# A hybrid decoder layer in float32 on one core: where the weight sums of the up projection are made, and the hand-over to the down projection

## The chip, the cores and the metric

The kernel runs on one core of a Trainium2 chip. A core has five engines that run side by side and meet only through semaphores: TensorE (PE in the profile, its weight loads PEld), VectorE (DVE), ScalarE (ACT), GpSimd (POOL) and SyncE (SP). Sixteen DMA engines move data between the chip's memory and the core's on-chip memory. Each engine takes its instructions in the order of its own queue.

The metric is the device time of one execution in microseconds (us). The profile is of one execution; its span runs from the first to the last instruction.

## The reference

One layer of a decoder on a residual stream of 1024 tokens by 1024 channels, all in float32: a norm and an input projection, a pooling mixer and a recurrent head group side by side, an output projection, a squared-ReLU MLP of width 4096, a gated embedding and a final norm.

```python
z = rms_norm(h, norm_mix_g[l])
proj = z @ w_in[l]
...
h = h + jnp.concatenate([y_pool, y_lru], axis=-1) @ w_out[l]
z = rms_norm(h, norm_mlp_g[l])
h = h + jnp.square(jax.nn.relu(z @ w_up[l])) @ w_down[l]
z = rms_norm(h, norm_ple_g[l])
gate = jax.nn.sigmoid(z @ w_ple_gate[l] + b_ple_gate[l])
h = h + gate * (p[l] @ w_ple_proj[l])
...
return rms_norm(h, norm_final_g)
```

The change lies in the MLP, the line with `w_up` and `w_down`.

## The kernel before, in words

**Arithmetic.** A float32 product is made from three passes of TensorE. Each operand is split into a high and a low part (`split`, lines 185 and 186: ScalarE copies the high part into the type that TensorE reads fast, VectorE subtracts it and leaves the low part), and TensorE adds high x high, high x low and low x high (`mm`, line 358).

**The up projection** works on 16 pairs of output tiles (`NPAIR`). For each pair the 2 x 2 block product of activations and weights is made with seven products instead of eight (the Strassen-Winograd scheme), called P1 to P7. Each product is four blocks of the contraction by three passes, 12 matmuls of 128x128 by 128x512. The scheme needs sums of the weight blocks A11, A12, A21 and A22 of each pair:

- P1 takes A11 and P2 takes A12 as they are, from the tile `a`; P4 takes A22 as it is, from a half of `T[5]`.
- P5 takes the running sum `chain` (the first half of the tile `c`), which starts as A21 + A22. Then A11 is added to it for P6, and then A12 for P3.
- P7 takes A21 + A11, the second half of `c`.

(The signs of the scheme are in the order of the blocks and in the sums of the activations.) In the kernel before, all four sums are made by DMAs that add what they read to what is already in the on-chip tile (`grow`, line 227). Such DMAs are issued by GpSimd (the queue POOLq), plain loads by SyncE (SPq).

**Loading.** `load_up(m)` issues, for pair m, the load of A21 into both halves of `c` (line 243), the accumulation of A22 and A11 onto them (512 KB), the load of A11 and A12 into `a` (line 248) and of A22 into `T[5]` (line 249). There are two sets of tiles `a` and `c`; for even pairs they come from a rotating pool (`wu_raw` in the profile), for odd pairs they are two fixed tiles (`wu`). In the kernel before, `load_up(m + 2)` is asked for at the split of P4 of pair m. For the last pair the weight of P3 has a tile of its own, `T[4]`, filled by one load and three accumulating DMAs (line 251 and `grow`).

**Order.** `UP` lists the products. From pair 2 on a pair runs P1, P5, P4 of the pair before (written P4' here), P6, P2, P3, P7. `weights()` hands out a split weight and asks for one further on in the list, so splits are made ahead of their products. The split weights take four slots in rotation (`up_place` and the two buffers of `wp`). The splits keep their order among themselves; the other instructions are placed by a scheduler, which also may put a DMA earlier than the source does.

**Within a pair** (`up_open`, `up_fourth`, `up_pair`): P1 goes to the bank `ps_a_u`, and a ScalarE copy (line 911) starts the bank `ps_b_u` with its negative, on which P6, P7 and later P4 are added. ScalarE copies of finished banks are at line 852, VectorE's subtractions at line 874. When P4 of a pair is done, `finish_up` applies ReLU, the norm's factor and the square (lines 833 and 835), makes the sums that the down projection's scheme needs (line 218) and stores everything to memory in four DMAs (lines 846 and 847).

**Last pair and the down projection.** `up_last` runs the last pair. On the way `preload_down` and `open_down` load the first weights (line 293) and the first operands `X` of the down projection (line 299, `wd<-act`). `open_down` gives up the space `y`, in which the operands of P1, P2 and P3 lie, and opens the space `wd` at its place; `X` are its first four tiles. A space opened like this waits for all readers of what lay there before. The down projection then runs 2 chunks of seven products by four parts, all of `ps_P_d`.

Of the kernel before, what the change touches and what calls it, by code (L numbers as in the profile page):

```python
# [8 lines left out]
F32 = mybir.dt.float32  # L9
# [3 lines left out]
ALU = mybir.AluOpType  # L13
# [35 lines left out]
NPAIR = DFF // P // 2  # L49
# [14 lines left out]
def block_kernel(  # L64
# [17 lines left out]
    nc = tc.nc  # L82
    pool = ctx.enter_context(tc.tile_pool(name="pool", bufs=1))
# [13 lines left out]
    A = [a_pair(i) for i in range(NT)]  # L97
    spaces = {}

    def space(name, n, dt, side="left"):  # L100

        spaces[name] = ExitStack()
        sb = spaces[name].enter_context(tc.tile_pool(name=name, bufs=1, side=side))
        return [sb.tile([P, S], dt, name=f"{name}{i}") for i in range(n)]

    def leave(name):
# [8 lines left out]
    T = [t_all[:, i] for i in range(6)]  # L115
# [16 lines left out]
    def bank(name):  # L132
        return pd.tile([P, HALF], F32, tag="pd", name=name)
# [4 lines left out]
    HALVES = FIRST, SECOND = slice(0, HALF), slice(HALF, S)  # L138
# [43 lines left out]
    def split(src, hi, lo, g=None, eng=None):  # L182

        if g is None:
            first = pin(nc.scalar.activation(hi, src, AF.Copy))  # L185
            lowest[:] = [pin((eng or nc.vector).tensor_tensor(lo, src, f32(hi), ALU.subtract)).ins]  # L186
        else:
            first = pin(nc.scalar.activation(hi, src, AF.Identity, scale=g))
            lowest[:] = [pin(nc.vector.scalar_tensor_tensor(lo, src, g, f32(hi), ALU.mult, ALU.subtract)).ins]
        upper[:] = [first.ins]  # L190
        return first.ins

    def raw_tile(name):
        return wp.tile([P, S], F32, tag="raw", name=f"{name}_raw")
# [22 lines left out]
    def dv(op, to, x, y):  # L217
        return nc.vector.tensor_tensor(to, x, y, op).ins

    up_raw, up_lower, up_spare, up_place = {}, {}, [], itertools.cycle(("whi", "wlo"))  # L220
    A22, A11, A12, A21 = (slice(n * HALF, (n + 1) * HALF) for n in range(4))

    def twice(x):
        return x.unsqueeze(1).broadcast_to([P, 2, x.shape[-1]])

    def grow(to, src):
        nc.gpsimd.dma_start(to, src, accum_op=ALU.add)
# [9 lines left out]
    def load_up(m):  # L237

        a, c = [raw_tile(f"wu{m}_{i}") for i in range(2)] if m % 2 == 0 else up_spare
        up_raw[m] = a, c, T[5][:, HALVES[m % 2]], c[:, FIRST] if m else R[:, SECOND]  # L240
        w = w_up[m]
        if m:
            nc.sync.dma_start(c.rearrange("p (y s) -> p y s", y=2), twice(w[:, A21]))
            grow(c, w[:, : 2 * HALF])
        else:
            nc.sync.dma_start(c[:, SECOND], w[:, A21])
            grow(c[:, SECOND], w[:, A11])
        nc.sync.dma_start(a, w[:, A11.start : A12.stop])
        nc.sync.dma_start(up_raw[m][2], w[:, A22])
        if m == NPAIR - 1:  # L250
            nc.sync.dma_start(T[4][:, FIRST], w[:, A21])
            for x in (A22, A11, A12):
                grow(T[4][:, FIRST], w[:, x])

    FIRST_UP = "P6", "P7", "P4", "P5", "P1", "P2", "P3"
    UP = [(0, kind) for kind in FIRST_UP]
    for m in range(1, NPAIR - 1):
        UP += [(m, "P1"), (m, "P5")] + [(m - 1, "P4")] * (m > 1) + [(m, kind) for kind in ("P6", "P2", "P3", "P7")]
    m = NPAIR - 1
    UP += [(m, "P1"), (m, "P5"), (m, "P2"), (m, "P3"), (m - 1, "P4"), (m, "P4"), (m, "P6"), (m, "P7")]  # L260

    def up_weight(m, kind):
        first, last = m == 0, m == NPAIR - 1
        if first and kind == "P6":
            load_up(0)
        a, c, a22, chain = up_raw[m]
        src = {
            "P1": a[:, FIRST], "P2": a[:, SECOND], "P4": a22, "P5": R[:, FIRST] if first else chain,
            "P6": chain, "P7": c[:, SECOND], "P3": T[4][:, FIRST] if last else chain,
        }[kind]  # L270
        w = wp.tile([P, S], F32R, tag=next(up_place), name=f"wu{m}_{kind}")
        hi, lo = (w[:, hs] for hs in HALVES)
        split(src, hi, lo)
        up_lower[m, kind] = lowest[0]
        if kind == "P5" and not first:
            grow(chain, w_up[m][:, A11])
        elif kind == "P6" and not last:
            grow(chain, w_up[m][:, A12])
        elif kind == ("P4", "P3")[first] and m < NPAIR - 2:
            load_up(m + 2)  # L280
        elif first and kind == "P7":
            load_up(1)
        return hi, lo

# [59 lines left out]
    def weights():  # L344
        ask()
        return asked.pop(0)
# [169 lines left out]
    for k in range(NT):  # L516
# [3 lines left out]
        for hs in halves:  # L520
            if k == hs.start == 0:
                whi, wlo = (t[:, :HALF] for t in weight_tiles("wl0"))
                g = col("g_mix", 0)
                x, zhi, zlo = (t[:, hs] for t in (H[0], *A[0]))
# [9 lines left out]
            x, zhi, zlo = (t[:, hs] for t in (H[k], *A[k]))  # L534
# [18 lines left out]
        if k < 2:  # L553

            zhi, zlo = A[k]
            for hs in HALVES:
# [4 lines left out]
                for n, o in kinds:  # L561
                    w, z = ((whi, zhi), (whi, zlo), (wlo, zhi))[n]
# [57 lines left out]
    def lru_gates(o):  # L620


        hi, lo = hl(0), hl(2)
        ct, rt, _ = LSETS[o % 2]
        zhi, zlo = B[4 + o]
        ps = [psum(f"ps_g{h}{o}") for h in range(2)]
        halves = [
            [(hs.start + n, x[:, n : n + HALF]) for hs, x in parts for n in range(0, hs.stop - hs.start, HALF)]
            for parts in ps
        ]  # L630
        for n, (w, z) in enumerate(((hi, zhi), (hi, zlo), (lo, zhi))):
            for (at, x0), (_, x1) in zip(*halves):
                for r, x in zip(HEADS, (x0, x1)):
                    nc.tensor.matmul(
                        x, w[r, o * P : (o + 1) * P], turns(z[r, at : at + HALF]), start=n == 0, stop=n == 2
                    )

        with tc.issue_after(newest[0]):
            for dst, b, rows in ((rt, "ga_b", HEADS), (ct, "gx_b", HEADS[::-1])):
                for h, r in enumerate(rows):  # L640
                    for hs, part in ps[h]:
                        last = nc.scalar.activation(
                            by(dst[HEADS[h], hs], part), got(part[r]), AF.Sigmoid, bias=col(b, o)[r]
                        )
        nc.vector.tensor_tensor(H[o], H[o], ct, ALU.mult)
        return last.ins
# [76 lines left out]
    last = lru_gates(1)  # L723
# [10 lines left out]
    last = lru_gates(3)  # L734
# [3 lines left out]
    last = lru_scan(1, last)  # L738
# [130 lines left out]
    def up_product(m, kind, ps, ts=range(4), w=None, more=False):  # L869
        product(ps, w or weights(), lambda t: up_operand(kind, t), ts, more=more)  # L870
# [33 lines left out]
    def up_open(m):  # L904

        cc, c11, c12, c21, c22 = up_sums(m)
        a, d = bank(f"ps_a_u{m}"), bank(f"ps_d_u{m}")
        up_product(m, "P1", a)
        if m < NPAIR - 1:
            chains[m] = banks(f"ps_b_u{m}")[:, :HALF]  # L910
            nc.scalar.activation(chains[m], a, AF.Copy, scale=-1.0)  # L911
        else:
            copy(c12, a)
        up_product(m, "P5", d)
        copy(c22, d)
        return a, d

    def up_fourth(m):
        cc, c11, c12, c21, c22 = up_sums(m)
        ps = chains.pop(m)  # L920
        up_product(m, "P4", ps, more=True)
        copy(c21, ps)
        return finish_up(m, cc)
# [21 lines left out]
    def up_last():  # L945
        m = NPAIR - 1
        cc, c11, c12, c21, c22 = up_sums(m)
        preload_down()
        a, d = up_open(m)
        up_product(m, "P2", a, more=True)  # L950
        copy(c11, a)
        up_product(m, "P3", d, more=True)
        first = open_down()
        store_up = up_fourth(m - 1)
        with tc.issue_after(first):
            store_up()
        ps = bank(f"ps_P4_u{m}")
        up_product(m, "P4", ps)
        load_w(0, 0, 3)
        copy(c21, ps)  # L960
        ps = bank(f"ps_P6_u{m}")
        up_product(m, "P6", ps)
        prepare(0, 0)
        take(c12, ps, c12)
        dv(ALU.subtract, c22, c12, c22)
        add(c21, c12)
        take(c12, d, c12)
        ps = banks(f"ps_P7_u{m}")[:, :HALF]
        up_product(m, "P7", ps)
        for tp in range(1, NQ):  # L970
            prepare(0, tp)
        add_both(cc[:, 1].rearrange("p (y s) -> p y s", y=2), ps)
# [8 lines left out]

    def open_down():
        leave("y")
        tiles = space("wd", 8, F32)
        late = space("wd1", 4, F32, "right")
        early.append(space("w0", 2, F32R))
        X[:] = tiles[:NQ]
        for q in range(NQ):
            W[1, q], W[3, q] = late[q], tiles[NQ + q]
        for tp in range(NQ):  # L990
            last = load_x(0, tp)
        load_w(0, 0, 2)
        for q in range(2):
            load_w(0, 1, q)
        return last.ins
# [330 lines left out]
    for g, hs in enumerate(GROUPS):  # L1326
# [3 lines left out]
        for n, o in enumerate(ORDER[g]):  # L1330
# [14 lines left out]
            if g == 0 and 1 <= n < 5:  # L1345
                raw = wp.tile([P, S], F32, tag="raw", name=f"wg0_{n + 3}_raw")
                nc.sync.dma_start(raw, w_gate[n + 3])
                x = slice((n - 1) * P, n * P)
# [142 lines left out]
```

## Time and profile before

| what | us |
|---|---|
| three runs: lowest, median, highest | 1016.5, 1017.62, 1021.67 |
| the profiled execution, its own time | 1016.62 |
| its span, first to last instruction | 1014.9 |
| mean TensorE clock granted | 0.972 of full |

How to read the profile: PE is TensorE's matmuls, PEld its weight loads, which lie beside them. L358 is line 358 of the kernel. `out<-in` names the tiles, with their numbers left out, so `ps_b_u` stands for the bank of every pair. An arrow with an engine and a line after an idle time names what ended that idle time. The number after the time in a group is the mean length of one instruction in ns.

The page also gives the span in 40 slices of 25.4 us, each digit the busy share of an engine in tenths (9 is 90% or more), PEclk the granted clock:

```profile
PE   9999999999797878787879799999999999999996
PEld 7888888888676757575667587888888888888885
DVE  7998885486544434343434369889987668888865
ACT  7469954374333423333333255443434344656322
POOL 4300001001111111101010100000000000000001
PEclk9999999999898989898989899999999999999999
```

The up projection lies in slices 9 to 24, the down projection in slices 25 to 36.

### The profile page before, as it was taken

The page shows a single profiled execution, that of the slowest core. Times are in us where ns is not written, and L with a number is a line of the kernel's source. Part 1 is how long each engine was busy: PE and PEld are TensorE (multiplying, and loading weights), DVE is VectorE, ACT ScalarE, POOL GpSimd, SP SyncE. Part 2 cuts the span into 40 slices and gives each one's busy share as a digit, 9 for nine tenths or more (in the row PEclk, how much of TensorE's full clock was granted, in tenths as well). Part 3 has the DMA queues.
Part 4 walks back from the last instruction along what each step waited for, and adds up shares of the span by engine and source line. Part 5 has one row for each costly group of instructions (what it writes and reads, how often), then busy time and mean ns, then how long its engine had stood idle before and what let it go on. Part 6 is the DMA issues. An engine that isn't in the chain of part 4 may idle for free.

```text
span 1014.9 us, 11314 instructions
## 1 busy us (share of the span) xinstructions
PE 939.7 (93%) x4227; PEld 802.5 (79%) x4227; DVE 681.8 (67%) x819; ACT 464.8 (46%) x606; POOL 68.8 (7%) x87
## 2 busy tenths in 40 slices
PE   9999999999797878787879799999999999999996
PEld 7888888888676757575667587888888888888885
DVE  7998885486544434343434369889987668888865
ACT  7469954374333423333333255443434344656322
POOL 4300001001111111101010100000000000000001
PEclk9999999999898989898989899999999999999999
DMA  7210263146665566566665679946653234013263
GB/s 255 84 52 32 83 200 96 46 100 153 163 187 166 167 165 166 166 166 165 166 166 166 165 238 335 341 146 187 217 193 125 83 125 146 21 64 103 54 192 117
DMA packets 61766, 151.38 MB, mean 149 GB/s; under 512 B 5520, under 2 KB 10512, under 8 KB 61712
## 3 DMA queue, kind: packets, MB, share of 16 engines
q1 hardware_dynamic: 54224, 133.10, 39.4%
q0 software_dynamic: 7488, 17.57, 10.6%
q8 instruction: 33, 0.54, 0.2%
q14 instruction: 21, 0.17, 0.1%
HBM read 114.99 MB, written 35.65 MB: 148 GB/s over the span
## 4 chain that ended last, share of the span: by engine, by line
PE 63%; DMA 21%; DVE 7%; issue 5%; ACT 3%; POOL 1%; SPq 0%; DVEq 0%; POOLq 0%; ACTq 0%
PE ps_P_d L358 28%; DMA wu<-in_w_up 10%; DMA wu_raw<-in_w_up 9%; PE ps_i L358 8%; PE ps_o L358 8%; PE ps_e L358 7%; DVE t_h L833 3%; PE ps_l L358 3%; DVE wu_P L186 2%; ACT wu_P L185 1%; PE ps_b_u L358 1%; ACT t_h L835 1%; PE ps_a_u L358 1%; PE ps_P_u L358 1%; PE ps_l L565 1%
## 5 line engine op out<-in xcount | busy, mean ns | idle before, releaser
L358 PE MATMUL ps_P_d<-a,wd_P_hi 128*128 128x512 f32 x880 | 261.7, 379 | 0.0
L358 PE MATMUL ps_b_u<-a,wu_P 128*128 128x512 f32 x504 | 135.7, 424 | 54.4 <-ACT ps_b_u L911 54.4
L358 PEld LDWEIGHTS ps_P_d<-a,wd_P_hi 128*128 128x128 f32 x880 | 166.3, 189 | 23.6
L358 PEld LDWEIGHTS ps_b_u<-a,wu_P 128*128 128x128 f32 x504 | 105.1, 213 | 79.2 <-ACT ps_b_u L911 59.7
L358 PE MATMUL ps_P_d<-a,wd_P_lo 128*128 128x512 f32 x440 | 166.8, 379 | 0.0
L186 DVE TENSOR_TENSOR wu_P<-wu_raw,wu_P 128x512 fp32r<-128x512 f32 x45 | 30.9, 688 | 103.3 <-ACT wu_P L185 103.3
L358 PEld LDWEIGHTS ps_P_d<-a,wd_P_lo 128*128 128x128 f32 x440 | 83.2, 189 | 11.8
L186 DVE TENSOR_TENSOR wu_P<-wu,wu_P 128x512 fp32r<-128x512 f32 x47 | 32.3, 687 | 80.2 <-ACT wu_P L185 80.2
L358 PE MATMUL ps_a_u<-y,wu_P 128*128 128x512 f32 x360 | 84.8, 384 | 0.0
L185 ACT ACTIVATE wu_P<-wu_raw 128x512 fp32r<-128x512 f32 x45 | 27.9, 621 | 116.6 <-DMA wu_raw<-in_w_up 116.3
L358 PEld LDWEIGHTS ps_a_u<-y,wu_P 128*128 128x128 f32 x360 | 68.3, 192 | 12.4 <-DVE wu_P L186 2.5
L185 ACT ACTIVATE wu_P<-wu 128x512 fp32r<-128x512 f32 x47 | 29.0, 621 | 93.5 <-DMA wu<-in_w_up 88.2
L186 DVE TENSOR_TENSOR a<-wd,a 128x1024 fp32r<-128x1024 f32 x56 | 67.2, 1219 | 1.8 <-ACT a L185 1.5
L358 PE MATMUL ps_i<-a,wi_hi 128*128 128x512 f32 x256 | 66.1, 381 | 0.0
L358 PE MATMUL ps_o<-y,wo_hi 128*128 128x512 f32 x256 | 65.7, 379 | 0.0
L815 DVE TENSOR_TENSOR t_h<-t_h,ps_P_d 128x512 f32<-128x512 f32 (+1 forms) x56 | 42.5, 759 | 34.0 <-PE ps_P_d L358 34.0
L185 ACT ACTIVATE a<-wd 128x1024 fp32r<-128x1024 f32 x56 | 58.1, 1049 | 13.1 <-PE ps_P_d L358 7.0
L358 PEld LDWEIGHTS ps_i<-a,wi_hi 128*128 128x128 f32 x256 | 48.1, 189 | 8.0 <-issue 0.7
L358 PEld LDWEIGHTS ps_o<-y,wo_hi 128*128 128x128 f32 x256 | 48.4, 189 | 6.9
L358 PE MATMUL ps_d_u<-y,wu_P 128*128 128x512 f32 x180 | 45.2, 397 | 9.2 <-ACT wu_P L185 6.3
L185 ACT ACTIVATE wd_P_hi<-wd 128x1024 fp32r<-128x1024 f32 x24 | 25.3, 1054 | 52.6 <-PE ps_P_d L358 52.5
L358 PEld LDWEIGHTS ps_d_u<-y,wu_P 128*128 128x128 f32 x180 | 34.1, 195 | 18.9 <-ACT wu_P L185 8.3
(263 smaller groups left out, 1572.4 us busy)
## 6 DMA issues: line engine op xcount, KB each, us to landing
wd<-act SPq DMA_DIRECT2D x56, 512.0 KB, 5.5
act<-t_h SPq DMA_DIRECT2D x32, 512.0 KB, 5.9
wu<-in_w_up SPq DMA_DIRECT2D x16, 512.0 KB, 5.0
act<-wu SPq DMA_DIRECT2D x16, 512.0 KB, 6.2
wd<-in_w_down SPq DMA_DIRECT2D x16, 512.0 KB, 5.8
wu_raw<-in_w_up SPq DMA_DIRECT2D x15, 512.0 KB, 5.4
t_h<-in_xT SPq DMA_DIRECT2D x14, 512.0 KB, 4.6
wg_raw<-in_w_gate SPq DMA_DIRECT2D x10, 512.0 KB, 3.3
```

What stands on the lines that cost most here:

```text
L185: first = pin(nc.scalar.activation(hi, src, AF.Copy))
L186: lowest[:] = [pin((eng or nc.vector).tensor_tensor(lo, src, f32(hi), ALU.subtract)).ins]
L358: ins = nc.tensor.matmul(ps, w, turns(z[:, hs]), start=first and z is zhi and w is whi, stop=last and w is wlo, skip_group_check=more,)
L565: nc.tensor.matmul(ps, kblk(w, o), turns(z[:, hs]), start=k == n == 0, stop=False)
L815: (eng or nc.vector).tensor_tensor(to, to if y is None else y, x, ALU.add)
L833: nc.vector.scalar_tensor_tensor(cc, cc, 0.0, twice(R), ALU.max, ALU.mult)
L835: nc.scalar.activation(x, x, AF.Square)
```

## The change

It touches the loading of the up projection's weights, the order of the last pair and the opening of the space `wd`.

- `load_up` no longer loads A22 except for the first two pairs; a new function `load_a22` does. `load_up(m + 2)` is asked for at the split of P7 of pair m (at P3 for the first pair), `load_a22(m + 2)` at the split of P4, as before.
- After the split of P5, VectorE adds A11 to `chain` from the tile `a`; after the split of P6 it adds A12. The two accumulating DMAs that did this are gone. The other two sums (A21 + A22 and A21 + A11) stay accumulating DMAs in `load_up`.
- For the last pair VectorE makes `T[4]` from `chain` and A12; its four DMAs are gone.
- In the last pair P4 of the pair before comes ahead of P2 and P3, and with it that pair's finish; the stores of that finish are still issued behind the loads of `X`.
- The space `wd` is opened with waits by tile instead of by pool: each of its tiles waits for the readers of what lay at its own place.

```diff
-    def space(name, n, dt, side="left"):
+    def space(name, n, dt, side="left", waits="pool"):
 
         spaces[name] = ExitStack()
-        sb = spaces[name].enter_context(tc.tile_pool(name=name, bufs=1, side=side))
+        sb = spaces[name].enter_context(tc.tile_pool(name=name, bufs=1, side=side, reuse_waits=waits))
         return [sb.tile([P, S], dt, name=f"{name}{i}") for i in range(n)]
...
         nc.sync.dma_start(a, w[:, A11.start : A12.stop])
-        nc.sync.dma_start(up_raw[m][2], w[:, A22])
-        if m == NPAIR - 1:
-            nc.sync.dma_start(T[4][:, FIRST], w[:, A21])
-            for x in (A22, A11, A12):
-                grow(T[4][:, FIRST], w[:, x])
+        if m < 2:
+            load_a22(m)
+
+    def load_a22(m):
+        nc.sync.dma_start(T[5][:, HALVES[m % 2]], w_up[m][:, A22])
...
-    UP += [(m, "P1"), (m, "P5"), (m, "P2"), (m, "P3"), (m - 1, "P4"), (m, "P4"), (m, "P6"), (m, "P7")]
+    UP += [(m, "P1"), (m, "P5"), (m - 1, "P4"), (m, "P2"), (m, "P3"), (m, "P4"), (m, "P6"), (m, "P7")]
...
         if kind == "P5" and not first:
-            grow(chain, w_up[m][:, A11])
+            dv(ALU.add, chain, chain, a[:, FIRST])
+            if last:
+                dv(ALU.add, T[4][:, FIRST], chain, a[:, SECOND])
         elif kind == "P6" and not last:
-            grow(chain, w_up[m][:, A12])
-        elif kind == ("P4", "P3")[first] and m < NPAIR - 2:
-            load_up(m + 2)
-        elif first and kind == "P7":
+            dv(ALU.add, chain, chain, a[:, SECOND])
+        if m < NPAIR - 2:
+            if kind == ("P7", "P3")[first]:
+                load_up(m + 2)
+            if kind == ("P4", "P3")[first]:
+                load_a22(m + 2)
+        if first and kind == "P7":
             load_up(1)
...
         a, d = up_open(m)
+        store_up = up_fourth(m - 1)
         up_product(m, "P2", a, more=True)
         copy(c11, a)
         up_product(m, "P3", d, more=True)
         first = open_down()
-        store_up = up_fourth(m - 1)
         with tc.issue_after(first):
             store_up()
...
         leave("y")
-        tiles = space("wd", 8, F32)
+        tiles = space("wd", 8, F32, waits="tile")
         late = space("wd1", 4, F32, "right")
```

## The prediction

> **What bounds the kernel now.** I began with the page's busy times: PE has 93% of the span, so only the places where it stands can give anything. Next came the windows of the stages: busy time of PE, its weight loads, VectorE, ScalarE and GpSimd in a stretch, then TensorE's clock, the DMA engines' share and GB/s.
>
> ```profile
> PE 939.7 (93%) x4227; PEld 802.5 (79%) x4227; DVE 681.8 (67%) x819; ACT 464.8 (46%) x606; POOL 68.8 (7%) x87
> ...
> core 0: us, PE busy (x) PEld busy (x) DVE busy (x) ACT busy (x) POOL busy (x), PEclk, DMA share, GB/s
> 224.60:608.36 383.76, 320.09 (x1350) 265.01 (x1349) 175.79 (x224) 140.53 (x231) 40.07 (x46) 0.93 0.64 171
> 448.98:498.10 49.12, 37.47 (x157) 30.63 (x155) 19.64 (x25) 15.54 (x27) 4.38 (x5) 0.93 0.65 171
> 585.00:600.00 15.00, 15.00 (x69) 12.67 (x69) 8.93 (x14) 9.02 (x15) 0.86 (x1) 1.00 0.68 213
> 600.50:615.00 14.50, 12.26 (x58) 10.41 (x57) 12.61 (x15) 8.88 (x10) 0.00 (x0) 1.00 0.91 324
> 614.20:901.00 286.80, 286.79 (x1329) 251.07 (x1330) 236.61 (x237) 130.63 (x141) 0.00 (x0) 1.00 0.50 164
> ```
>
> The down stage (the last row) is dense: 286.80 / 1329 = 0.2158 us a matmul. The up stage (from 224.60) is not. Its 16 pairs hold 16 x 7 products x 12 matmuls = 1344, and with 4 matmuls of the norm 1348 x 0.2158 = 290.9 us. It takes 383.76, so 92.9 us are lost there. The row from 448.98 is two pairs, 24.56 us each, where 84 x 0.2158 = 18.1 would do. A dense product is 12 x 0.2158 = 2.59.
>
> Who makes PE wait is in the groups by line and form of TensorE (busy, mean ns, idle before, releaser) and in the waits:
>
> ```profile
> L358 PE MATMUL ps_b_u<-a,wu_P 128*128 128x512 f32 x504 | 135.7, 424 | 54.4 <-ACT ps_b_u L911 54.4
> L358 PE MATMUL ps_d_u<-y,wu_P 128*128 128x512 f32 x180 | 45.2, 397 | 9.2 <-ACT wu_P L185 6.3 <-ACT t_h L852 2.8
> ACT wu_P L185 <- DMA wu_raw<-in_w_up: 116.3, 14, 13.2
> ACT wu_P L185 <- DMA wu<-in_w_up: 88.2, 13, 9.5
> ```
>
> PE names a ScalarE copy (L911), but that copy reads a product long finished. One pair in the timeline shows why it is late (start, duration, in brackets the idle time before):
>
> ```profile
> 406.61 0.38 SPq L243 DMA_DIRECT2D wu<-in_w_up  x1
> 407.10 1.99 SPq L846 DMA_DIRECT2D act<-t_h  x2
> 411.71 0.32 SPq L846 DMA_DIRECT2D act<-wu  x1
> 412.13 0.88 POOL L227 DMA_DIRECT2D wu<-in_w_up  x1 [14.19 <-DVE wu L218]
> 412.69 1.23 POOL L227 DMA_DIRECT2D wu_raw<-in_w_up  x1
> 414.25 2.75 PE L358 MATMUL ps_b_u<-a,wu_P 128*128 128x512 f32 x12
> 422.67 0.63 ACT L185 ACTIVATE wu_P<-wu_raw 128x512 fp32r<-128x512 f32 x1 [12.61 <-DMA wu_raw<-in_w_up]
> 423.20 0.58 ACT L911 ACTIVATE ps_b_u<-ps_a_u 128x512 f32<-128x512 f32 x1
> 423.83 4.91 PE L358 MATMUL ps_b_u<-a,wu_P 128*128 128x512 f32 x12 [6.83 <-ACT ps_b_u L911]
> 446.29 2.86 PE L358 MATMUL ps_b_u<-a,wu_P 128*128 128x512 f32 x12 [2.00 <-ACT ps_b_u L911]
> ```
>
> The sum for P6 (chain + A11) is an accumulating DMA on GpSimd's queue. At 412.13 that queue serves the 512 KB sum of a later pair, and this pair's sum comes behind it at 412.69. ScalarE sits on the P6 split until 422.67, with L911 behind it in its queue, and PE with both. So **the up stage is bound by the landing of accumulating DMAs inside the pair**.
>
> The loss has two halves. Idle before matmuls is 54.4 + 9.2 = 63.6 us; the other 29.3 are slow matmuls after a stall. After 6.83 us idle, twelve take 4.91; after 2.00 they take 2.86, near the dense 2.75. Here the Trainium skill bears ("TensorE: Matmul & The Clock Gate", section "What's actually happening"): about 3.4 us idle halves the clock until PE has been busy as long, and the trace agrees with its 4.91 and 2.86.
>
> **The change, part by part.**
>
> *Two sums on VectorE.* Both in-pair accumulating DMAs go (two in each of pairs 1 to 14, one in the last: 29). In their place stand 30 VectorE additions of 128x512 from tiles already in SBUF. Their nearest row is the same shape on the same engine:
>
> ```profile
> L218 DVE TENSOR_TENSOR wu<-t_h 128x512 f32<-128x512 f32 x16 | 11.0, 685 | 0.0
> ```
>
> So 2 x 0.69 = 1.4 us a pair. VectorE does 19.64 us in two pairs; with the additions 22.4 of 36.3, or 62%. They are covered by VectorE's idle time if they run early. They can: four weight slots rotate, so a split may start once the product four places before it has ended. At a dense PE, P5's split may start 5.2 us before its pair, the first addition follows at once, and P6's split may start at 0, when P6 itself is due at 7.8. P3's split may start at 5.2 and P3 is due at 12.9. Without that cover, the chain split, subtract, add (0.63 + 0.69 + 0.69 = 2.0 us) twice would be bare: 4.0 us a pair.
>
> *The load a pair ahead.* The DMAs for pair m+2 (the first half's twofold load, its 512 KB accumulation on GpSimd, and the A11/A12 tile) are now asked for at P7 of pair m instead of P4 of m in the next pair. A22 alone stays with P4. Prices, from the DMA issues (count, KB, us to landing), from the view of these tiles, and VectorE's longest instruction from the timeline:
>
> ```profile
> wu<-in_w_up SPq DMA_DIRECT2D x16, 512.0 KB, 5.0
> wu<-in_w_up POOLq DMA_DIRECT2D x8, 512.0 KB, 8.5
> DMA to landing us min/median/max: 3.2/5.9/10.4
> ...
> 403.69 2.29 DVE L833 SCALAR_TENSOR_TENSOR t_h<-t_h,rstd 128x2048 f32<-128x2048 f32 x1
> ```
>
> With t = 0 at the pair's P1, P7's split starts at 7.8 (P4' has ended) and, behind a 2.29 us VectorE instruction, ends by about 12. The load lands at 12.4 + 5.0 = 17.4, the accumulation at 17.4 + 0.9 + 8.5 = 26.8. P5 of m+2 must begin to split at 36.3 + 2.6 - 1.3 = 37.6. That is **10.8 us of slack**; with both landings at the longest seen, 10.4, still 3.9. So DMA latency leaves the path. On SP the loads pass the four stores of a pair's finish. At 406.61 SP already issues the load ahead of those stores, so I cost the move at 0; at worst SP holds them from 407.10 to 411.71, 4.6 us, which the slack covers. On GpSimd's queue only one accumulation a pair is left, so none stands behind another.
>
> *Bytes.* Two pairs moved 49.12 us x 171 GB/s = 8.40 MB; four 256 KB sums fewer make 7.35 MB, in 36.3 us 203 GB/s. The row 585 to 600 shows 213 GB/s at a clock of 1.00 and a share of 0.68. No bound.
>
> *The last pair's sum, T[4].* Four DMAs become one VectorE addition. Before, the scheduler put them early, in the way of pair 1:
>
> ```profile
> 248.33 0.86 POOL L227 DMA_DIRECT2D t_h<-in_w_up  x1 [4.28 <-DMA t_h<-in_w_up]
> 248.89 1.20 POOL L227 DMA_DIRECT2D wu<-in_w_up  x1
> 256.87 4.54 PE L358 MATMUL ps_d_u<-y,wu_P 128*128 128x512 f32 x12 [2.76 <-ACT t_h L852]
> ```
>
> Pair 1's second sum stood behind one of them, and P3 of pair 1 started late by 2.76. This is inside the 92.9.
>
> *Last pair reordered, space handed over tile by tile.* P4' moves ahead of P2 and P3. The first down operands (X) overlay the tiles that P1 and P2 read.
>
> ```profile
> 595.41 2.75 PE L358 MATMUL ps_d_u<-y,wu_P 128*128 128x512 f32 x12
> 598.00 2.75 PE L358 MATMUL ps_b_u<-a,wu_P 128*128 128x512 f32 x12
> 598.19 1.90 SPq L299 DMA_DIRECT2D wd<-act  x3
> 608.36 2.97 PE L358 MATMUL ps_P_d<-a,w 128*128 128x512 f32 x13
> 611.20 1.22 DVE L218 TENSOR_TENSOR wu<-t_h,wu 128x1024 f32<-128x1024 f32 x1
> 614.21 1.56 PE L358 MATMUL ps_P_d<-a,w 128*128 128x512 f32 x6 [2.24 <-DVE a L186]
> ```
>
> Before, the X loads waited for the end of P3 (598.0), with four products, 10.4 us, to the down stage. After, they can go during P2, with P3, P4, P6, P7 and part of P2 to come: 10.4 to 12 us. Without the tile-wise wait the reorder would leave three products, 7.8. The stores and sums of pair 14 (the 611.20 row) also come two products earlier, out of the way of the X splits. What they delayed is the stop after 16 matmuls: 608.36 + 16 x 0.2158 = 611.8 to 614.21, 2.4 us. If the X loads do not move, in the busiest stretch of the DMAs (share 0.91), these 2.4 stay.
>
> **The sum.** 92.9 + 2.4 = 95.3 us can go. I leave 1.0 at the start of down and 2.3 in the stage for waits that a dense stage still has; the weight loads' short waits for VectorE's half of a split bound these:
>
> ```profile
> PEld ps_b_u L358 <- DVE wu_P L186: 2.7, 8, 0.3
> PEld ps_d_u L358 <- DVE wu_P L186: 2.6, 6, 0.4
> PEld ps_a_u L358 <- DVE wu_P L186: 2.5, 8, 0.3
> ```
>
> They are 7.8 together, 0 at the other end, and I take the part nearer to 0, since splits would run three products ahead. That saves 92.0. The profiled execution took 1016.62 (span 1014.9 and 1.7 around it), 1.0 under the median of the three runs. Forecast: 1016.6 - 92.0 = **924.6 us**.
>
> **The rivals.**
>
> *The stall shrinks but stays (0.24).* Something in the in-order queues still comes late each pair: ScalarE, whose splits, copies and squares share one queue, or the X-to-VectorE-to-ScalarE chain of the sums. For it: the bare chain is 4.0 us, and L911 has only the 5.2 us of P5 and P4' as cover. Against it: ScalarE does 15.54 us in two pairs, under half of 36.3, and its long waits were all for DMAs. With 2.0 us a pair over 14 pairs, 28: 953. With 4.0, 56, and the clock falls too: at 4.91 against 2.75 that is 2.2 a pair more, 87 together, 1012. By the rule of the Trainium skill named above, only gaps over its window pay this second part.
>
> *The stall only changes its place (0.04).* If P5 waits for its load as long as P6 did for its sum, the time stays within 0.5%, 1012 to 1022. Against it: the slack of 10.8 us.
>
> *Slower: the load falls behind the stores of the wrong pair (0.06).* SP serves in order, and the order is the scheduler's. If the load for m+2 stands behind the four stores of pair m itself, which can't be ready until P4' in pair m+1, each pair becomes a loop: P4' ends, 8.0 us of finish (403.69 to the last store at 411.71), 14.4 of load and accumulation, 1.3 of split, P5 and P4', 5.2. That is 28.9 us a pair against 24.56: 14 x 4.3 = 61 us slower, some 1078, with slow matmuls more. It decides once SP issues the load over 24.56 - 14.4 - 1.3 - 5.2 = 3.7 us after P4' has ended. Against it: at 406.61 SP issued the load before the stores although the source asked for it later than now.
>
> *The handover does nothing:* 2.4 of the sum stay; within the forecast's own range.
>
> **How the numbers follow.** Forecast 0.66 (range of its own 917 to 936: all 95.3 gone is 921.3, and runs of this kernel spread by some us; above, the 7.8 and the 2.4 stay). The range must take most of the first rival too, to about 958 (just over 2 us a pair); that leaves out the upper part of it, 0.08, and the last two, 0.10: 917 to 958. Half a per cent, 5 us, is about what a measurement of this kernel tells from no change. Faster by more: 0.66 + 0.24 = 0.90; within: 0.04; slower: 0.06.
>
> **What the profile will show.** If right: the up stage takes about 293 us, its clock reads 1.00, the wait of PE for L911 is under 5 us, ScalarE's waits for weights from w_up are nearly gone, VectorE's group of additions has 30 more, GpSimd one accumulation a pair, and the first down product starts without a stop over 1 us. Wrong if PE still waits before P6 or P5: the releaser then tells whether a DMA (load too late), VectorE (the additions) or L911 (ScalarE's order) holds it. If SP's load row stands after the stores of its pair, the third rival holds.

## The result, and the profile after

The changed kernel takes **923.38 us** (median of 4 runs, 922.97 to 923.71); the kernel before took 1017.06 beside it (4 runs, 1014.89 to 1021.67). The ratio is 0.9073 (95%: 0.9041 to 0.9105). The forecast was 924.6, in the range 917 to 958. The profiled execution took 923.41, its span is 921.6.

The page's busy times and the windows of the changed kernel, with the columns of the prediction's first fence; the windows are the whole up stage and two pairs of it:

```profile
PE 911.9 (99%) x4227; PEld 792.9 (86%) x4227; DVE 701.7 (76%) x850; ACT 468.9 (51%) x606; POOL 38.0 (4%) x54
...
225.26:517.17 291.91, 291.47 (x1349) 254.72 (x1348) 197.91 (x259) 147.78 (x235) 12.12 (x14) 1.00 0.70 197
400.00:436.30 36.30, 36.30 (x170) 31.80 (x169) 23.25 (x30) 17.27 (x29) 1.73 (x2) 1.00 0.76 203
```

The up stage fell from 383.76 to 291.91 us, PE stands in it for 0.44 us in all, and its clock reads 1.00 where it read 0.93. Two pairs take 36.3 us where they took 49.12. VectorE went from 67% to 76% of the span with no more than 20 us of new work: the span got shorter.

| part of the span | before | after | saved |
|---|---|---|---|
| ahead of the up stage | 224.60 | 225.26 | -0.66 |
| up stage | 383.76 | 291.91 | 91.85 |
| the stop in the first 24 matmuls of down | 2.40 | 0.56 | 1.84 |
| the rest | 404.14 | 403.87 | 0.27 |
| span | 1014.9 | 921.6 | 93.3 |

Three groups of the up stage by line and form, and then, from the waits (time, number, longest), ScalarE's in the up stage and TensorE's only one there:

```profile
L363 PE MATMUL ps_b_u<-a,wu_P 128*128 128x512 f32 x504 | 113.5, 379 | 0.0
...
L363 PE MATMUL ps_d_u<-y,wu_P 128*128 128x512 f32 x180 | 41.3, 379 | 0.0
L363 PE MATMUL ps_P_u<-a,wu_P 128*128 128x512 f32 x84 | 19.0, 382 | 0.4 <-DVE wu_P L186 0.4
```
```profile
ACT ps_b_u L916 <- PE ps_a_u L363: 26.7, 14, 1.9
ACT wu_P L185 <- PE ps_b_u L363: 26.1, 13, 2.0
...
ACT wu_P L185 <- DMA wu<-in_w_up: 0.7, 1, 0.7
...
PE ps_P_u L363 <- DVE wu_P L186: 0.4, 1, 0.4
```

The 54.4 us that PE spent on the copy L911 (now L916) are gone, and the mean of its matmuls fell from 424 to 379 ns. The direction of the waits has turned: ScalarE spent 204 us on DMAs of `w_up` ahead of a split, and now 0.7; its splits and copies wait for PE instead. That is how a bound that has moved to TensorE reads.

One pair in the timeline (start, duration, in brackets the idle time before), from four engines:

```profile
404.90 0.68 DVE L218 TENSOR_TENSOR wu_raw<-wu_raw,wu_raw 128x512 f32<-128x512 f32 x1
```
```profile
406.05 0.63 ACT L185 ACTIVATE wu_P<-wu_raw 128x512 fp32r<-128x512 f32 x1 [2.01 <-PE ps_b_u L363]
408.60 0.58 ACT L916 ACTIVATE ps_b_u<-ps_a_u 128x512 f32<-128x512 f32 x1 [1.91 <-PE ps_a_u L363]
```
```profile
405.81 2.75 PE L363 MATMUL ps_a_u<-y,wu_P 128*128 128x512 f32 x12
408.39 2.75 PE L363 MATMUL ps_d_u<-a,wu_P 128*128 128x512 f32 x12
410.99 5.34 PE L363 MATMUL ps_b_u<-a,wu_P 128*128 128x512 f32 x24
```
```profile
404.69 0.86 POOL L227 DMA_DIRECT2D wu<-in_w_up  x1 [23.35 <-DMA act<-t_h]
416.23 0.87 POOL L227 DMA_DIRECT2D wu_raw<-in_w_up  x1 [10.67 <-DMA wu_raw<-in_w_up]
```

The pair starts at 405.81. VectorE has added A11 at 404.90, before P1; P6 is split at 406.05, and TensorE runs P4' and P6 as 24 matmuls without a break from 410.99. GpSimd issues one accumulation a pair. VectorE has 31 instructions more than before (850 against 819), one more than the forecast's 30: pair 0 has an A12 sum too, which that count left out.

The start of the down stage:

```profile
517.17 4.48 PE L363 MATMUL ps_P_d<-a,w 128*128 128x512 f32 x19
521.83 1.35 PE L363 MATMUL ps_P_d<-a,w 128*128 128x512 f32 x5 [0.17 <-DVE a L186]
```
```profile
505.06 2.56 SPq L304 DMA_DIRECT2D wd<-act  x4
```

The `X` loads go at 505.06, 12.1 us ahead of the stage. 19 matmuls end at 517.17 + 19 x 0.2158 = 521.27, the next starts at 521.83: a stop of 0.56, where 2.40 were. (The row's own 0.17 is the idle time that the trace shows; the same kind of row had 2.24 before.) So each sign that the prediction named for its forecast is there.

### The profile page after: what moved, and what is told of

Read it like the earlier page. It is cut to its first block, busy times and chain, and to the rows that moved or that the text cites. A ratio compares the mean times of both kernels' runs of the same rounds, so it can differ in the third digit from the quotient of the medians.

```text
span 921.6 us, 11220 instructions
## 1 busy us (share of the span) xinstructions
PE 911.9 (99%) x4227; PEld 792.9 (86%) x4227; DVE 701.7 (76%) x850; ACT 468.9 (51%) x606; POOL 38.0 (4%) x54
## 4 chain that ended last, share of the span: by engine, by line
PE 93%; DVE 3%; issue 1%; DMA 1%; ACT 0%; SPq 0%; DVEq 0%; POOLq 0%; POOL 0%
PE ps_P_d L363 31%; PE ps_b_u L363 12%; PE ps_i L363 9%; PE ps_a_u L363 8%; PE ps_d_u L363 8%; PE ps_o L363 8%; PE ps_e L363 8%; PE ps_l L363 3%; PE ps_P_u L363 1%; PE ps_l L570 1%; PE ps_j L363 1%; DVE y L189 1%; PE ps_g L639 1%; PE ps_e L1243 1%; PE ps_p L363 1%
## 5 line engine op out<-in xcount | busy, mean ns | idle before, releaser
L363 PE MATMUL ps_b_u<-a,wu_P 128*128 128x512 f32 x504 | 113.5, 379 | 0.0
L363 PEld LDWEIGHTS ps_b_u<-a,wu_P 128*128 128x128 f32 x504 | 95.3, 189 | 13.5
L363 PE MATMUL ps_a_u<-y,wu_P 128*128 128x512 f32 x360 | 82.6, 379 | 0.0
L186 DVE TENSOR_TENSOR a<-wd,a 128x1024 fp32r<-128x1024 f32 x56 | 67.0, 1217 | 0.9 <-ACT a L185 0.6
L838 DVE SCALAR_TENSOR_TENSOR t_h<-t_h,rstd 128x2048 f32<-128x2048 f32 x16 | 36.7, 2291 | 19.3 <-ACT t_h L857 19.3
L186 DVE TENSOR_TENSOR wu_P<-wu,wu_P 128x512 fp32r<-128x512 f32 x47 | 32.3, 686 | 22.2 <-ACT wu_P L185 22.2
L186 DVE TENSOR_TENSOR wu_P<-wu_raw,wu_P 128x512 fp32r<-128x512 f32 x45 | 30.8, 687 | 23.6 <-ACT wu_P L185 23.6
L363 PE MATMUL ps_d_u<-a,wu_P 128*128 128x512 f32 x180 | 41.3, 379 | 0.0
L363 PE MATMUL ps_d_u<-y,wu_P 128*128 128x512 f32 x180 | 41.3, 379 | 0.0
```

Source lines behind the costliest of these rows:

```text
L363: ins = nc.tensor.matmul(ps, w, turns(z[:, hs]), start=first and z is zhi and w is whi, stop=last and w is wlo, skip_group_check=more,)
L838: nc.vector.scalar_tensor_tensor(cc, cc, 0.0, twice(R), ALU.max, ALU.mult)
```

## The experiments

The theory: the 92 us of the up stage are the two accumulating DMAs inside each pair, and the other edits add the 2 us at the end. The rivals: the load a pair ahead carries part of it; the additions on VectorE or the place of the load cost something that only chance hides; the end owes its gain to the order alone.

### One edit alone

**The sums on VectorE, nothing else** (the kernel before, with the loads, `T[4]` and the end as they were):

```diff
-            grow(chain, w_up[m][:, A11])
+            dv(ALU.add, chain, chain, a[:, FIRST])
...
-            grow(chain, w_up[m][:, A12])
+            dv(ALU.add, chain, chain, a[:, SECOND])
```

> The kernel before with only the two sums (A11 and A12) of pairs 1 to 15 on VectorE; loads asked for at P4 as before, T[4] still by four DMAs, last pair and hand-over as before. Theory (the in-pair accumulating DMAs are the bound, through ScalarE's queue): nearly the whole gain, 924 to 932 us, what is missing being the end of the stage (about 2) and T[4]'s DMAs in pair 1 (0 to 5). Rival (the load a pair ahead is what counts): P5 waits for its load, over 950. Rival (T[4]'s DMAs in the way are what counts): over 1000.

Measured: 924.45 us (922.83 to 926.33), ratio 0.9099 (0.9072 to 0.9127). Two lines carry nearly the whole gain. What is left is the stop at the start of down, in the group of its first matmuls:

```profile
L358 PE MATMUL ps_P_d<-a,w 128*128 128x512 f32 x24 | 5.8, 384 | 2.1 <-DVE a L186 2.1
```

**The load a pair ahead, nothing else** (the kernel before, with `load_up` asked for at P7):

```diff
-        elif kind == ("P4", "P3")[first] and m < NPAIR - 2:
-            load_up(m + 2)
...
+            if kind == ("P7", "P3")[first]:
+                load_up(m + 2)
+            if kind == ("P4", "P3")[first]:
+                load_a22(m + 2)
```

> The kernel before with only the loads asked for at P7 of pair m instead of P4. Every engine's queue comes out instruction by instruction as in the kernel before, since the scheduler had put these loads at the same places already. Theory: 1015 to 1021, as before. Rival (the load a pair ahead carries part of the gain): under 1000.

Measured: 1014.84 us, in one execution; the up stage takes 383.80 us at a clock of 0.93, as before. On all five queues the instructions stand in the same order as in the kernel before. The scheduler had already put these loads where the edit asks for them.

**The whole change with the load asked for at P4 again:**

```diff
-            if kind == ("P7", "P3")[first]:
+            if kind == ("P4", "P3")[first]:
                 load_up(m + 2)
```

> The changed kernel with the loads asked for at P4 as before, all else kept. Its queues come out the same as the changed kernel's, instruction by instruction. Theory (that edit does nothing): 922.5 to 924.5. Rival (asking earlier matters): slower by over 5.

Measured: 922.92 us (922.81 to 923.82), ratio 0.9095 (0.9064 to 0.9125), again with the queues of the changed kernel, instruction by instruction. Beside the sums, too, the edit of the load does nothing.

### One sum back to its DMA

**A12 by DMA**, in the changed kernel:

```diff
-            dv(ALU.add, chain, chain, a[:, SECOND])
+            grow(chain, w_up[m][:, A12])
```

> The changed kernel with one of the two sums back as an accumulating DMA: + A12 for P3 (pairs 1 to 14). Theory (what does not fit into a pair is the two accumulations one after the other, ahead of L911): with P6's split done at about t = 1.4 of its pair, 0.9 to issue and 5.6 to 6.6 to land make 9, up to 12 behind another accumulation, where P3's split is due at 11.6: little or no stall, 923 to 945. Rival (each in-pair accumulation costs half the loss): about 970.

Measured: 947.88 us (947.36 to 948.27), ratio 0.9338 (0.9323 to 0.9354): 24.5 more than the change, a little above the upper end. The wait is where it was expected, before P3 (the group on `ps_d_u` with `y`):

```profile
L363 PE MATMUL ps_d_u<-y,wu_P 128*128 128x512 f32 x180 | 48.4, 410 | 11.9 <-ACT wu_P L185 11.5
```

**A11 by DMA:**

```diff
-            dv(ALU.add, chain, chain, a[:, FIRST])
+            grow(chain, w_up[m][:, A11])
```

> The changed kernel with the other sum back as an accumulating DMA: + A11 for P6 (pairs 1 to 15). Theory: P5's split done at about t = -3.9, 0.9 and 5.6 to 6.6 make 3 to 4, up to 7 behind another accumulation, where P6's split is due at 6.5, and L911 stands behind it on ScalarE: 0 to 2 us of stall a pair, 923 to 952. Rival (each in-pair accumulation costs half the loss): about 970.

Measured: 957.74 us (954.79 to 959.42), ratio 0.9433 (0.941 to 0.9456): 34.4 more than the change, again above the upper end. Its timeline on VectorE, GpSimd, ScalarE and TensorE, in two pairs; in the second the 512 KB accumulation of a later pair is just ahead on GpSimd's queue:

```profile
399.66 0.69 DVE L186 TENSOR_TENSOR wu_P<-wu,wu_P 128x512 fp32r<-128x512 f32 x1
...
419.07 0.68 DVE L186 TENSOR_TENSOR wu_P<-wu_raw,wu_P 128x512 fp32r<-128x512 f32 x1
```
```profile
400.70 0.89 POOL L227 DMA_DIRECT2D wu<-in_w_up  x1 [1.94 <-DVE wu_P L186]
421.51 0.87 POOL L227 DMA_DIRECT2D wu<-in_w_up  x1 [19.92 <-DVE t_h L879]
422.09 1.18 POOL L227 DMA_DIRECT2D wu_raw<-in_w_up  x1
```
```profile
409.46 0.63 ACT L185 ACTIVATE wu_P<-wu 128x512 fp32r<-128x512 f32 x1 [9.55 <-DMA wu<-in_w_up]
...
431.79 0.63 ACT L185 ACTIVATE wu_P<-wu_raw 128x512 fp32r<-128x512 f32 x1 [12.45 <-DMA wu_raw<-in_w_up]
```
```profile
410.63 2.86 PE L363 MATMUL ps_b_u<-a,wu_P 128*128 128x512 f32 x12 [1.02 <-ACT ps_b_u L916]
...
432.95 4.54 PE L363 MATMUL ps_b_u<-a,wu_P 128*128 128x512 f32 x12 [3.92 <-ACT ps_b_u L916]
```

The L186 rows end P5's split. In the first pair A11's sum is issued right behind it, at 400.70 (the 512 KB accumulation had gone out at 397.90); P6's split starts 8.8 us later, and PE stands for 1.02. In the second pair P5's split has ended at 419.75, but the sum stands on GpSimd behind the other accumulation until 422.09, and from there to P6's split at 431.79 are 9.7 us; PE stands for 3.92. Counted from each pair's P1 (401.68 and 421.10) the issue is 2.0 us later, and the sum then takes 0.9 longer: together the 2.9 us by which the two stops differ. I had reckoned with the median landings of the kernel before, 5.6 and 6.6 us. In these two runs the medians of the same transfers are 6.7 and 8.1 (A12), 8.1 and 9.0 (A11). Together the two single DMAs cost 24.5 + 34.4 = 58.9 us, the pair of them 92: more than the sum of the parts. A likely reason, not tried by itself: with both, A12's is issued only after A11's has landed and P6 is split, so the second starts late by the whole of the first.

**The in-pair DMAs kept, the load's accumulation taken away** (the kernel before; A21 + A22 and A21 + A11 are made by VectorE ahead of P1's split, A11 and A12 are still added by DMA):

```diff
-            grow(c, w[:, : 2 * HALF])
...
+        if kind == "P1" and not first:
+            dv(ALU.add, chain, chain, a22)
+            dv(ALU.add, c[:, SECOND], c[:, SECOND], a[:, FIRST])
```

> The kernel before with the other two sums on VectorE (A21 + A22 and A21 + A11, made just ahead of P1's split) and the two in-pair sums left as accumulating DMAs: GpSimd's queue has two accumulations a pair, none of 512 KB, none of another pair in the way. Theory A (the two accumulations in sequence do it alone): P5's split done at -3.9, 0.9 + 7 to 8.3 to land (as the trace with A12 alone shows), split 1.3, again 0.9 + 7 to 8.3, make 13.2 to 15.8 where P3's split is due at 11.6: 1.6 to 4.2 a pair and slow matmuls, 950 to 1000. Theory B (the queue on GpSimd, an accumulation of a later pair ahead of this pair's, does most): under 950. If neither: about 1017.

Measured: 971.75 us (970.33 to 974.03), ratio 0.9574 (0.9532 to 0.9616), between the two kernels. Two pairs on TensorE:

```profile
402.99 4.38 PE L360 MATMUL ps_b_u<-a,wu_P 128*128 128x512 f32 x12 [2.64 <-ACT ps_b_u L913]
...
425.03 2.86 PE L360 MATMUL ps_b_u<-a,wu_P 128*128 128x512 f32 x12 [2.12 <-ACT ps_b_u L913]
```

PE's wait for the copy is 22.2 us in all, against 54.4. So the two in-pair DMAs by themselves cost some 49 us (971.75 less 922.91, which is the time with all four sums on VectorE, below, in the same series; in it are also some 2 us of the old end, which this kernel keeps), and the accumulation of a later pair beside them another 42 (1013.76, the kernel before in that series, less 971.75). This run takes away both that accumulation's place on GpSimd's queue and its traffic; which of the two weighs more stays open here. In the pair with A11 by DMA above, 2.0 us came from the place on the queue and 0.9 from the longer transfer.

### The cover of the additions

**Each addition tripled** (add, subtract, add), 4 two-input instructions a pair more on VectorE:

```diff
-            dv(ALU.add, chain, chain, a[:, FIRST])
+            for op in (ALU.add, ALU.subtract, ALU.add):
+                dv(op, chain, chain, a[:, FIRST])
...
-            dv(ALU.add, chain, chain, a[:, SECOND])
+            for op in (ALU.add, ALU.subtract, ALU.add):
+                dv(op, chain, chain, a[:, SECOND])
```

> The changed kernel with each of the two sums made as add, subtract, add on VectorE: four more 0.69 us instructions a pair, in the chain of the sums, 2.7 us a pair. Theory (VectorE is covered: 12.4 of 18.1 us, with these 15.1): 923 to 926. Rival (the bare chain of splits and sums sets the pair): 14 x 2.7 = 38 more, about 961.

Measured: 924.3 us (923.47 to 924.64), ratio 0.9105 (0.9087 to 0.9123).

**All four sums on VectorE**, in the changed kernel, with the same edit as in the kernel before that has no accumulating load:

> The changed kernel with all four sums of pairs 1 to 15 on VectorE: no accumulating DMA is left in those pairs, two more 0.69 us additions a pair (VectorE 13.8 of 18.1 us). Theory (PE is the bound now): 922 to 925. Rival (the additions right ahead of P5's split come on the path): 930 or more.

Measured: 922.91 us (922.73 to 923.93), ratio 0.9095 (0.9064 to 0.9125). Two pairs of the two kernels in the windows, the tripled additions first, then the four sums:

```profile
300.00:336.26 36.26, 36.26 (x170) 31.75 (x169) 28.20 (x38) 17.29 (x29) 1.72 (x2) 1.00 0.69 200
```
```profile
300.00:336.26 36.26, 36.26 (x170) 31.80 (x169) 25.66 (x34) 17.23 (x29) 0.00 (x0) 1.00 0.52 171
```

PE has 36.26 of 36.26 us in both, with VectorE at 28.20 (78%) and with the DMA engines' share at 0.69 or 0.52. The additions lie wholly beside TensorE. Taking the last accumulations away gains nothing that can be measured: 922.91 stands beside the 922.92 and 923.38 of two kernels that keep them.

### Where the load's slack ends

**The load of pair m + 2 behind the stores of pair m - 1** (only SP's order changes):

```diff
-            if kind == ("P7", "P3")[first]:
+            if kind == "P3" and first:
                 load_up(m + 2)
...
-            up_fourth(m - 1)()
+            stored = up_fourth(m - 1)()
...
+        if m < NPAIR - 2:
+            with tc.issue_after(stored) if stored else ExitStack():
+                load_up(m + 2)
```

> The changed kernel with the load of pair m+2 queued on SP behind the last stores but one of pair m-1's finish; only SP's order differs. The twofold load goes 5 to 12 us later. Theory (some 10 us of slack for the odd pairs, more for the even): 923 to 926. Rival (the load's landing is on the path): 14 x 5 us or more, over 990.

Measured: 923.74 us (923.03 to 923.83), ratio 0.9099 (0.9085 to 0.9114). SP issues the loads behind the stores:

```profile
400.07 2.00 SPq L851 DMA_DIRECT2D act<-t_h  x2
...
403.35 0.40 SPq L243 DMA_DIRECT2D wu<-in_w_up  x1
```

**The load of pair m + 1 behind the same stores**, that is a pair later:

```diff
-            if kind == ("P7", "P3")[first]:
+            if kind == "P3" and first:
                 load_up(m + 2)
...
-            up_fourth(m - 1)()
+            with tc.issue_after(up_fourth(m - 1)()):
+                load_up(m + 1)
```

> The changed kernel with the load of pair m+1 queued on SP behind the stores of pair m-1's finish, one pair later than now (13 loads, pairs 3 to 15). Theory (the prediction's loop of the slower rival): P4' to P4' becomes 8.0 of finish, 14.4 of load and accumulation, 1.3 of split and 5.2 of P5 and P4' = 28.9 us a pair in place of 18.1, 13 x 10.8 = 140 more, and up to 2.2 a pair of slow matmuls: 1064 to 1093. If loads have slack for a whole pair: 923.

Measured: 1053.21 us (2 runs, 1052.89 and 1053.52), ratio 1.0376 (1.0323 to 1.043): slower than the kernel before, and 11 us under the expected band. Its SP queue, ScalarE and TensorE:

```profile
417.40 0.46 SPq L243 DMA_DIRECT2D wu_raw<-in_w_up  x1
417.95 0.77 SPq L248 DMA_DIRECT2D wu_raw<-in_w_up  x1
```
```profile
425.73 0.63 ACT L185 ACTIVATE wu_P<-wu_raw 128x512 fp32r<-128x512 f32 x1 [10.75 <-DMA wu_raw<-in_w_up]
```
```profile
426.42 5.43 PE L363 MATMUL ps_a_u<-y,wu_P 128*128 128x512 f32 x12 [6.88 <-ACT wu_P L185]
```

Now it is P1 that waits, for the plain load of A11, 6.88 us, and its matmuls are slow behind the stop. 13 pairs are 1053.2 - 923.4 = 129.8 us longer, 10.0 each, on 18.1: 28.1 us a pair.

### The end

**The order of the last pair and the opening of `wd` as before**, the rest of the change kept:

```diff
-        store_up = up_fourth(m - 1)
         up_product(m, "P2", a, more=True)
...
         first = open_down()
+        store_up = up_fourth(m - 1)
...
-        tiles = space("wd", 8, F32, waits="tile")
+        tiles = space("wd", 8, F32)
```

> The changed kernel with the last pair's order and the hand-over as before (space wd waits by pool). Theory: the stop after the first down matmuls comes back, 1.8 us: 925 to 926. Rival (the end brings nothing, the X loads are bound by the DMAs there): 923.4, within 0.5.

Measured: 925.47 us (924.06 to 926.12), ratio 0.9109 (0.9088 to 0.9129): 2.1 more than the change, with a stop of 1.93 in the first down matmuls:

```profile
L363 PE MATMUL ps_P_d<-a,w 128*128 128x512 f32 x24 | 7.1, 447 | 1.9 <-DVE a L186 1.9
```

Beside the first experiment it differs on the queues only in `T[4]`, which is four DMAs there (924.45) and one addition here: the DMAs of `T[4]` cost nothing once no in-pair DMA stands behind them.

**The new order with the old waits by pool:**

```diff
-        tiles = space("wd", 8, F32, waits="tile")
+        tiles = space("wd", 8, F32)
```

> The changed kernel with its new order in the last pair, but space wd waiting by pool: the same queues, only the waits differ. Theory: the X loads wait for the end of P3, three products (7.8 us) ahead of the down stage instead of 12 us as in the changed kernel's trace, 4.3 us later; the stop grows by 3 to 4.3: 926 to 928. Rival (the order alone is enough): 923.4, within 0.5.

Measured: 924.67 us (924.01 to 925.08), ratio 0.9102 (0.9083 to 0.9121): 1.3 more than the change, less than expected. Its `X` loads and the start of down:

```profile
509.48 2.62 SPq L304 DMA_DIRECT2D wd<-act  x4
```
```profile
521.04 1.56 PE L363 MATMUL ps_P_d<-a,w 128*128 128x512 f32 x6 [0.78 <-DVE a L186]
523.10 1.35 PE L363 MATMUL ps_P_d<-a,w 128*128 128x512 f32 x5 [0.49 <-DVE a L186]
```

The loads go 4.4 us later than with tile-wise waits, and PE stops for 0.78 and 0.49, where the changed kernel's row has 0.17. By these two runs the tile-wise wait is worth 1.3 us and the reorder the other 0.8 of the 2.1. But the kernel with the sums alone has the same old end and stands only 1.1 above the change (924.45): its first matmuls keep their length (384 ns in the mean), while with the old end in the changed kernel they are slow (447). So the times don't settle how the gain divides. The stops do show the order: 1.93 and 2.15 with the old end, 1.27 with the new order, 0.17 with both edits.

## Why the prediction was right

The forecast was 1.2 us high, and its likeliest case is the one that came. Step by step:

- **The bound** was read rightly: PE named a copy on ScalarE, ScalarE was held by a split, the split by an accumulating DMA. The edit that takes away those DMAs alone gives 924.45. The reading also named the accumulation of another pair ahead on GpSimd's queue; with all accumulations of the load gone, 42 of the 92 us go, though the in-pair DMAs stay.
- **The size, 92.9 removable and 2.3 left in the stage.** The stage takes 291.91, so 291.91 - 290.9 = 1.0 is left, 0.4 of it PE's wait for VectorE's half of a split. The 2.3 was picked between 0 and 7.8, not worked out, so that it came within 1.3 of the measured is in part luck. The 29.3 us of slow matmuls went with the stops, as they had to for this sum.
- **The cover of the additions** was costed at nothing, with VectorE at 62%. It stands at 23.25 of 36.3, 64%, and tripling the additions costs nothing.
- **The load a pair ahead** was costed at 0 on SP's queue, and that held. But "So DMA latency leaves the path" credited this edit with something that it doesn't do: the load already stood there in the kernel before, and alone or taken back it leaves every queue as it was. The row at 406.61, where SP issued the load ahead of the stores "although the source asked for it later than now", had said so. (The prediction's 3.9 us of slack with both landings at the longest is 3.5 when it is worked from 12.4, as the line before it is.) The slack is there: loads 3.9 and 10.7 us later (403.35 and 421.44 against the matching places of the changed kernel) cost nothing.
- **Bytes:** 203 GB/s forecast, 203 measured in the two pairs, and no bound at 171 or 203.
- **`T[4]`** was counted inside the 92.9, for its place ahead of pair 1's second sum. It is a cost only beside an in-pair DMA: the kernel without the load's accumulation, which keeps both, still has the wait of P3 of pair 1, 2.9 us.
- **The end.** Forecast 1.4 saved of 2.4, measured 1.84. The step that was mis-sized is the worth of the tile-wise wait: the sum asked for 10.4 to 12 us of lead where the reorder alone leaves 7.8, but with the 7.6 us that it left (509.48 to the stage's start at 517.05) the stop is already down to 1.3 by the trace's idle time, from 2.24.
- **The rivals.** The stall that stays didn't come in any form. The slower one didn't either, but its mechanism is real: forced on purpose, it gives 28.1 us a pair, where the working had 28.9. The wait falls on P1 and its plain load, not on P5 and its accumulation as the loop was drawn, and the 28.1 hold slow matmuls that the 28.9 leave out, so the nearness of the two is in part luck.

One rule of the Trainium skill was weighed in the prediction ("TensorE: Matmul & The Clock Gate", section "What's actually happening"), that about 3.4 us of idle time halves the clock. It agreed with the two rows quoted there, after 6.83 and 2.00 us. It doesn't agree with the row of pair 1, 4.54 us after 2.76, nor with the kernel without the load's accumulation, 4.54 us after 2.09, below. What the traces share with it is the length: two stretches at half clock, below, last 3.41 us. The forecast did not hang on it; it bore only on the second part of the first rival's upper case, 2.2 us a pair.

## What to carry to other kernels

When PE waits for a copy that has all its inputs, look at what stands ahead of the copy in its engine's queue: here the idle time was booked on a line that no edit needed to touch. A sum whose operand already lies in the on-chip memory is better made by an engine with idle time than by an accumulating DMA inside a loop's critical sequence; here that was worth 92 of 1017 us. And before a gain is credited to an earlier place in the source, compare the order of the queues: a scheduler may have put the work there already.

## What was not expected of the hardware

**The length of a stop alone did not decide whether the clock fell.** Two rows of the kernel without the load's accumulation stand above: 4.38 us after a stop of 2.64, and 2.86 after 2.12. Here is another of the same kernel, and then one of the kernel before:

```profile
337.32 4.54 PE L360 MATMUL ps_b_u<-a,wu_P 128*128 128x512 f32 x12 [2.09 <-ACT ps_b_u L913]
```
```profile
498.21 2.86 PE L358 MATMUL ps_b_u<-a,wu_P 128*128 128x512 f32 x12 [3.12 <-ACT ps_b_u L911]
```

So the product is slow after 2.09 and 2.64 us, and not slow after 2.12 and 3.12. Windows of the kernel without the load's accumulation show the clock (the third number from the right), first over the matmuls behind 2.64 and 2.12 us, then over two stretches at half clock:

```profile
402.99:407.20 4.21, 4.21 (x12) 3.46 (x13) 1.39 (x3) 0.97 (x2) 0.87 (x1) 0.63 0.47 84
425.03:427.70 2.67, 2.67 (x12) 2.37 (x13) 1.39 (x3) 0.97 (x2) 0.86 (x1) 1.00 0.11 19
...
337.85:341.26 3.41, 3.41 (x9) 2.69 (x8) 0.85 (x2) 0.44 (x1) 0.86 (x1) 0.50 0.49 73
402.70:406.11 3.41, 3.12 (x7) 2.52 (x8) 1.68 (x3) 1.26 (x3) 0.87 (x1) 0.50 0.27 37
```

Both stretches last 3.41 us, and they begin 64.85 us apart, 19 times 3.41 to within 0.1. So the clock looks as if it were set in fixed stretches of 3.41 us, and where a stop falls on them counts beside its length; what is counted within a stretch is not shown here. The slow product costs 4.38 - 2.86 = 1.5 us besides the stop. Behind the longer stops shown above it took 4.54 us (after 3.92), 4.91 (after 6.83) and 5.43 (after 6.88).

**The same 256 KB accumulation takes between 4.2 and 9.7 us from issue to the split that waits for it.** The windows from issue to split for A11's sum of one pair and A12's of the next in the kernel without the load's accumulation, where no other accumulation is under way (the DMA engines' share is the number before the last):

```profile
394.20:401.80 7.60, 6.15 (x29) 4.92 (x27) 3.18 (x5) 0.00 (x0) 0.89 (x1) 1.00 0.95 298
...
425.60:429.80 4.20, 4.20 (x21) 3.69 (x20) 0.82 (x2) 0.40 (x1) 0.83 (x1) 1.00 0.58 139
```

It takes 7.6 us where the DMA engines are busy to 95% and 4.2 where they are busy to 58%. With A11 by DMA it takes 8.8 when another accumulation has been issued 2.8 us ahead (400.70 to 409.46), and 9.7 when one has been issued 0.6 us ahead (422.09 to 431.79). That the traffic beside it makes the difference is likely, but no run varied the traffic alone. The expectations of both single sums came out low because they took the medians of the kernel before, in which A11's and A12's transfers stand in one group.
